# Weight-block sums made by accumulating loads: one step of a hybrid encoder layer

## The chip, the cores and the metric

The kernel runs on one core of one Trainium2 chip. A core has TensorE (PE) for matrix products, VectorE (DVE), ScalarE (ACT) and GpSimd (POOL) for everything else, SyncE (SP) for issuing transfers, and 16 DMA engines that carry them. The metric is the device time of one execution in microseconds. Before the change three runs took 2252.02, 2252.3 and 2253.97 us; the median is 2252.3 us.

## The reference: one layer of a streaming encoder

The input is x with 1024 frames of 1024 channels. One layer is computed, followed by a final RMSNorm:

1. h = RMSNorm(x), and one wide projection of h gives the columns for two branches. Branch A is a gated DeltaNet (8 heads of 128, short causal convolution, chunked delta rule). Branch B is gated linear attention, GLA (4 heads, keys of 128, values of 256, chunked). Each branch has a gated RMSNorm and a projection to 1024 channels, the two are merged by sigmoid gates, and an output projection adds the result to x.
2. x += cross attention of RMSNorm(x) over 256 memory tokens, 4 heads.
3. x += W2 relu(W1 RMSNorm(x))^2 with 4096 hidden channels.

All is float32. The large matrix products carry nearly all of the work: the projections of both branches, the output of the attention, and the two MLP products.

## The kernel before, in words

**Accuracy by splitting.** A float32 operand is split into a high half in a reduced type that TensorE takes at its fast rate (`fp32r`) and the rest, the low half. A product is then three matmuls: high by high, high by low, low by high (`mm3`, lines 487, 489 and 491). `split` does the splitting: ACT copies the high half (line 527), and DVE or POOL subtracts it from the raw value (line 528).

**Seven products for eight.** Many large products are done with Winograd's form of Strassen's scheme: both operands are taken as 2 x 2 blocks, and seven block products take the place of eight. For that, sums of blocks of both operands are needed, and sums of the results. The weight operand has blocks A11, A12, A21, A22, and the seven products use A11, A12, S2 = A21 + A22 - A11, S1 = A21 + A22, A22 - S2, A12 - S2 and A22. A *unit* is one such group of seven: per product 4 x 3 matmuls of 128x128 by 512 columns. `wino_w` (line 1551) prepares the weight operands of one unit, or of a pair of units: it makes four sums per unit, in place on the raw tiles (lines 1563, 1564, 1566 and 1568), and splits each into an operand tile. `wino` (line 1590) and `gla_dense` (line 861) issue the matmuls and hand the results to an `evict` function, which makes the sums of results out of PSUM: `into` (line 828), `sums` (line 1605) and `into_x` (line 1644). There are 39 units: 11 in the GLA stage (two of them with value weights in blocks of 256 columns), 8 for the two branch projections, 4 for the folded output of the attention, and 16 for the MLP's up projection.

**Tiles and rings.** Raw weights are loaded by SP into a ring of `RAWS = 4` tiles of 4 KB per partition named raw, and the split operands go into a ring of `RING = 4` tiles named wop. `queue_w` (line 1527) and `queue_gla` (line 1032) list the loads in order, `fetch_w` (line 1539) issues the next. A unit's raw tile holds 4 chunks of rows by 256 columns, so that a block is a strided half of it.

**The MLP's down projection** (`phase_mlp`, line 1964) is seven products over 15 chunks of rows, done in five passes: product 0, product 1, products 2 and 3, products 4 and 5, product 6. `weights` (line 2021) prepares one chunk of one pass, three steps ahead of the matmuls: for products 2 and 3 it loads blocks 0, 2 and 3, makes two sums (lines 2037 and 2038) and stores S2 to device memory (w2d); for products 4 and 5 it loads w2d and blocks 1 and 3 and makes two differences (lines 2043 and 2044). A step of two products is 24 matmuls of 512 columns.

**The order of the work.** The program is first written down as a plain trace, and a planner (`Plan`, line 131) then simulates all engines with a cost for each instruction and writes an order for each queue by list scheduling. An operation that adds or subtracts two tiles in SBUF may be moved between DVE and POOL by the planner (`Either`, line 399). A DMA costs 60 ns of its issuing engine there and lands after its bytes at 300 per ns plus 2600 ns (line 104). The queues of the engines are executed in the order that the planner wrote; only semaphores hold them back.

**Descriptors.** The kernel is built with `dynamic_dma_scratch_size=512` (line 2298), the bytes of each partition that are set aside for the descriptors of loads issued by GpSimd. Before the change there are no such loads.

Of the kernel before, what the change touches and what calls it, by code (L numbers as in the profile page):

```python
# [18 lines left out]
P = 128  # L19
# [54 lines left out]
class Op:  # L74
# [5 lines left out]
    def __init__(self, ins, flex):  # L80
# [343 lines left out]
class Layer:  # L424
# [206 lines left out]
    def phase0(self, xp):  # L631
        nc, a = self.nc, self.a
        with ExitStack() as ctx:
# [62 lines left out]
            def fold_o(h):  # L696
                vT = kv["wv"]
                w = [self.wpart(a["wo"][h][:, :, i * HALF:(i + 1) * HALF], [2, HALF], (None, nc.vector)[i], sp) for i in range(2)]
                for half in range(2):
                    for mb in range(2):  # L700
# [6 lines left out]
                        nc.scalar.activation(st.rearrange("p a b -> p (a b)"), pt, AF.Copy, scale=rm[0][:, mb:mb + 1])  # L707
                        nc.scalar.dma_start(self.Ud[:, 2 * half:2 * half + 2, mb, h], st)

# [118 lines left out]
    def into(self, dest, scale=1.0, done=None):  # L828

        nc = self.nc  # L830

        def add(o, pt, x):
            if scale == 1.0:
                nc.vector.tensor_tensor(o, pt, x, ADD)
            else:
                nc.vector.scalar_tensor_tensor(o, pt, scale, x, MUL, ADD)
# [690 lines left out]
    def queue_w(self):  # L1527
# [6 lines left out]
        q += [(4, [[g[:, 0:4], g[:, 4:8]]]) for g in self.Gd]  # L1534
        q += [(4, [[self.Ud[:, u, i] for i in range(2)] for u in us]) for us in pairs]
        q += [(4, [a["w1"][u] for u in us]) for us in [(0, 1)] + [(u,) for u in range(2, 14)] + [(14, 15)]]
        self.wq = deque(q)

    def fetch_w(self):
# [5 lines left out]
        for src in srcs:  # L1545
            rs.append([self.til(self.wp, [P, n, 256], "raw", bufs=RAWS) for _ in src])
            for t, x in zip(rs[-1], src):
                self.load(t, x)
        self.wr.append((n, rs))

    def wino_w(self, order, lov):

        nc, wp = self.nc, self.wp
        if not self.wr:
            self.fetch_w()
        n, rs = self.wr.popleft()
        ops = [{} for _ in rs]
        bl = [r if len(r) == 4 else [r[j][:, :, i * P:(i + 1) * P] for i in range(2) for j in range(2)] for r in rs]

        for p in order:  # L1560
            for o, (A11, A12, A21, A22) in zip(ops, bl):
                if p == 2:
                    nc.gpsimd.tensor_tensor(A21, A21, A22, ADD)
                    nc.gpsimd.tensor_tensor(A11, A21, A11, SUB)
                if p == 4:
                    nc.gpsimd.tensor_tensor(A21, A22, A11, SUB)
                if p == 5:
                    nc.gpsimd.tensor_tensor(A12, A12, A11, SUB)
                if A11.shape[-1] == P:
                    t = self.til(wp, [P, 2, n, P], "wop", F32R, bufs=RING)  # L1570
                    o[p] = t[:, 0], t[:, 1]
                else:
                    o[p] = [self.til(wp, [P, n, 256], "wop", F32R, bufs=RING) for _ in range(2)]
                self.split((A11, A12, A11, A21, A21, A12, A22)[p], *o[p], nc.vector if p in lov else None)
        return n, ops

    def plain_w(self):

        if not self.wr:
            self.fetch_w()  # L1580
        n, (r,) = self.wr.popleft()
        ops = {}
        for i in range(2):
            for j in range(2):
                t = ops[i, j] = self.til(self.wp, [P, 2, n, P], "wop", F32R, bufs=RING)
                self.split(r[j][:, :, i * P:(i + 1) * P], t[:, 0], t[:, 1])
        self.fetch_w()
# [17 lines left out]
    def sums(self, sp, done):  # L1605
# [6 lines left out]
        def evict(p, pt):  # L1612
# [9 lines left out]
            elif p == 2:  # L1622
                if "b" not in t:
                    t["b"] = self.til(sp, [P, HALF], "q", bufs=4)
                    nc.scalar.activation(t["b"], t["u"], AF.Copy)
                add(t["u"], pt, t["u"], ADD)
            elif p == 3:
# [16 lines left out]
    def into_x(self, sp, u, scale=1.0, done=None, tag="q", eng=None, up=None):  # L1644
# [16 lines left out]
        def evict(p, pt):  # L1661
# [8 lines left out]
            elif p == 2:  # L1670
                add(t["u"], pt, t["u"])
            elif p == 3:
# [291 lines left out]
    def phase_mlp(self, sp):  # L1964
# [56 lines left out]
        def weights(n):  # L2021
# [3 lines left out]
            ps, k = steps[n]  # L2025
            src = {(0,): "0", (1,): "1", (2, 3): "023", (4, 5): "S13", (6,): "3"}[ps]
            r = {}
            for i in range(0, len(src), 2):
                raw = self.til(self.wp, [P, 2, HALF], "raw", bufs=RAWS)
                for j, q in enumerate(src[i:i + 2]):  # L2030
                    r[q] = raw[:, j]
                    self.load(raw[:, j], self.w2d[k] if q == "S" else a["w2"][int(q), :, k])
            if len(src) == 1:
                ws = [r[src]]
            elif ps[0] == 2:

                nc.gpsimd.tensor_tensor(r["2"], r["2"], r["3"], ADD)
                nc.gpsimd.tensor_tensor(r["0"], r["2"], r["0"], SUB)
                nc.sync.dma_start(self.w2d[k], r["0"])
                ws = [r["0"], r["2"]]  # L2040
            else:

                nc.gpsimd.tensor_tensor(r["3"], r["3"], r["S"], SUB)
                nc.gpsimd.tensor_tensor(r["1"], r["1"], r["S"], SUB)
                ws = [r["3"], r["1"]]
# [103 lines left out]
    def run(self):  # L2149
# [5 lines left out]
        self.Gd = [dt([P, NB, 256], f"Gd{h}") for h in range(XH)]  # L2155
        self.Ud = dt([P, 4, 2, 4, 256], "Ud")
        self.md = [dt([P, 2, HALF], f"md{b}") for b in range(4)]
# [68 lines left out]
def _pairs(w):  # L2226

    return w.reshape(4, 2, P, -1, 256).transpose(3, 1, 2, 0, 4)

# [7 lines left out]
def _layout(i):  # L2237
# [9 lines left out]
                                             for h in range(LH)])])  # L2247
    A["w_lv"] = _pairs(w[:, lv])
    A["w_lr"] = _pairs(w[:, lr])
# [63 lines left out]
```

## Time and profile before

| | |
|---|---|
| median of three runs | 2252.3 us |
| lowest and highest | 2252.02 and 2253.97 us |
| span of the profiled execution, first to last instruction | 2248.6 us |
| median of the runs less that span | 3.7 us |
| TensorE busy | 2175.6 us, 97% |
| VectorE busy | 1668.2 us, 74% |
| ScalarE busy | 1101.5 us, 49% |
| GpSimd busy | 374.6 us, 17% |
| bytes moved by DMA | 300.20 MB, 134 GB/s on the mean |
| mean granted TensorE clock | 0.985 |

The profile is of one execution. Times are in us from the first instruction. A row of a group names the line of the kernel, the engine, the operation and its tiles (out<-in), their shape and the count; then come busy time and mean duration, or the shortest, median and longest duration. Matmuls are pipelined, so that the shown duration of one (0.39 us at 512 columns) is longer than the distance to the next. A row of waits says who waited for whom, how long in total, how often, and the longest. The landing time of a DMA is counted from its issue.

### The profile page before, as it was taken

The numbers are of one execution on the slowest core, as the hardware profiler recorded it, in microseconds if no ns is written. First come the engines' busy times: TensorE is split into PE (matmuls) and PEld (weight loads), VectorE is DVE, ScalarE is ACT, GpSimd is POOL, SyncE is SP. The second block draws the span as 40 slices with busy tenths as digits, with TensorE's granted clock in tenths as the row PEclk, the third lists the DMA queues.
The fourth block names the chain that finished last, engine by engine and source line by source line (L and its number), as shares of the span: only waits on it lengthen the run. The fifth ranks groups of instructions, "written<-read, shape, count | busy, mean of one in ns | idle before, by whom it ended". The sixth has DMA issues, their size and how long they took to land.

```text
span 2248.6 us, 32239 instructions
## 1 busy us (share of the span) xinstructions
PE 2175.6 (97%) x11552; PEld 1856.5 (83%) x11552; DVE 1668.2 (74%) x2901; ACT 1101.5 (49%) x2223; POOL 374.6 (17%) x326
## 2 busy tenths in 40 slices
PE   7899999989899999999998999999999999999996
PEld 7888979878788888888886888998888888888885
DVE  8836898687948858768558994558998778666756
ACT  6534554445445455355444433455665556544433
POOL 2100221022212222221111230002331002000012
PEclk9999999999999999999999999999999999999998
DMA  7932112122202102111167682244454445777732
GB/s 262 304 124 72 58 72 81 38 74 87 66 20 94 52 29 89 48 58 58 41 223 253 200 281 82 95 138 140 126 203 149 160 154 186 259 242 268 256 119 80
DMA packets 148463, 300.20 MB, mean 134 GB/s; under 512 B 15816, under 2 KB 22344, under 8 KB 148304
## 3 DMA queue, kind: packets, MB, share of 16 engines
q1 hardware_dynamic: 141504, 289.75, 38.6%
q10 hardware_dynamic: 6800, 8.42, 1.1%
q8 instruction: 90, 1.47, 0.3%
q14 instruction: 69, 0.57, 0.1%
HBM read 212.35 MB, written 85.75 MB: 133 GB/s over the span
## 4 chain that ended last, share of the span: by engine, by line
PE 83%; DVE 11%; issue 3%; ACT 2%; DMA 1%; POOL 0%; SPq 0%; DVEq 0%; ACTq 0%; POOLq 0%
PE pd L487 19%; PE pd L491 19%; PE pd L489 19%; PE ps L487 5%; PE ps L491 5%; PE ps L489 5%; PE ps L559 2%; DVE Pm L1223 1%; PE ps L1256 1%; DVE acc L1117 1%; DVE pr L1221 1%; PE ps L1247 1%; PE ps L1313 1%; PE ps L1296 1%; DVE wlo L528 1%
## 5 line engine op out<-in xcount | busy, mean ns | idle before, releaser
L527 ACT ACTIVATE wop<-raw 128x512 fp32r<-128x512 f32 (+1 forms) x444 | 297.1, 675 | 516.7 <-PE pd L491 242.9
L528 DVE TENSOR_TENSOR wop<-raw,wop 128x512 fp32r<-128x512 f32 (+1 forms) x387 | 297.3, 775 | 138.9 <-ACT wop L527 131.3
L1117 DVE SCALAR_TENSOR_TENSOR acc<-cin,convw,acc 128x1024 f32<-128x1024 f32 x72 | 96.8, 1345 | 7.9 <-ACT acc L1115 7.0
L527 ACT ACTIVATE whi<-raw 128x512 fp32r<-128x512 f32 x86 | 51.9, 627 | 92.3 <-PE pd L489 33.5
L528 POOL TENSOR_TENSOR wlo<-raw,whi 128x512 fp32r<-128x512 f32 x36 | 53.3, 1485 | 214.4 <-ACT whi L527 187.3
L491 PE MATMUL pd<-t,wop 128*128 128x512 f32 x220 | 88.9, 404 | 0.0
L487 PE MATMUL pd<-t,wop 128*128 128x512 f32 x220 | 86.9, 395 | 0.8 <-ACT t L527 0.8
L489 PE MATMUL pd<-t,wop 128*128 128x512 f32 x220 | 86.4, 393 | 0.7 <-DVE t L528 0.7
L491 PE MATMUL pd<-B1a,wop 128*128 128x512 f32 (+1 forms) x220 | 82.6, 376 | 0.0
L487 PE MATMUL pd<-B1a,wop 128*128 128x512 f32 (+1 forms) x220 | 82.6, 375 | 0.0
L528 POOL TENSOR_TENSOR wop<-raw,wop 128x512 fp32r<-128x512 f32 x23 | 33.0, 1434 | 271.2 <-ACT wop L527 260.5
L487 PE MATMUL pd<-A0a,whi 128*128 128x512 f32 x172 | 69.7, 405 | 0.0
L491 PE MATMUL pd<-A0a,wlo 128*128 128x512 f32 x172 | 69.0, 401 | 0.2 <-DVE wlo L528 0.2
L487 PE MATMUL pd<-A1b,whi 128*128 128x512 f32 x172 | 69.0, 401 | 0.0
L491 PE MATMUL pd<-A1b,wlo 128*128 128x512 f32 x172 | 68.6, 399 | 0.0
L489 PE MATMUL pd<-A1a,whi 128*128 128x512 f32 x172 | 68.6, 399 | 0.0
L489 PE MATMUL pd<-A0b,whi 128*128 128x512 f32 x172 | 68.2, 397 | 0.0
L487 PE MATMUL pd<-A1a,whi 128*128 128x512 f32 x172 | 68.1, 396 | 0.0
L491 PE MATMUL pd<-A1a,wlo 128*128 128x512 f32 x172 | 67.9, 395 | 0.0
L487 PE MATMUL pd<-A0b,whi 128*128 128x512 f32 x172 | 67.7, 393 | 0.0
L489 PE MATMUL pd<-A0a,whi 128*128 128x512 f32 x172 | 67.6, 393 | 0.0
L491 PE MATMUL pd<-A0b,wlo 128*128 128x512 f32 x172 | 67.6, 393 | 0.0
(623 smaller groups left out, 7163.3 us busy)
## 6 DMA issues: line engine op xcount, KB each, us to landing
raw<-in_w_dram SPq DMA_DIRECT2D x120, 256.0 KB, 3.5
raw<-in_w_gdn_dram SPq DMA_DIRECT2D x64, 256.0 KB, 2.7
raw<-in_w_dram SPq DMA_DIRECT2D x32, 512.0 KB, 4.0
e<-ad SPq DMA_DIRECT2D x63, 256.0 KB, 4.9
ad<-q SPq DMA_DIRECT2D x45, 256.0 KB, 2.8
rawa<-ad SPq DMA_DIRECT2D x42, 256.0 KB, 4.4
A0b<-tgd SPq DMA_DIRECT2D x32, 256.0 KB, 5.1
ad<-acc SPq DMA_DIRECT2D x30, 256.0 KB, 2.4
```

Of the source, the lines that this page charges most:

```text
L487: nc.tensor.matmul(out, lh, rh, start=first and i == 0, stop=False)
L489: nc.tensor.matmul(out, lh, rl, start=False, stop=False)
L491: nc.tensor.matmul(out, ll, rh, start=False, stop=last and i == n - 1)
L527: nc.scalar.activation(hi, raw, AF.Copy)
L528: (lo_eng or nc.gpsimd).tensor_tensor(lo, raw, hi.bitcast(F32), SUB)
L559: self.nc.tensor.transpose(pt[:, i * P:(i + 1) * P], s, self.ident)
L1117: nc.vector.scalar_tensor_tensor(acc, cin[:, 1 + i:1 + i + T], cw[:, i:i + 1], acc, MUL, ADD)
L1221: nc.vector.tensor_tensor(pr, X[:, c + 1:32, c:c + 1].broadcast_to([P, m, n]), Pm[:, c:c + 1, 0:n].broadcast_to([P, m, n]), MUL)
L1223: nc.vector.tensor_tensor(Pm[:, c + 1:32, 0:n], Pm[:, c + 1:32, 0:n], pr, ADD)
L1247: nc.tensor.matmul(pt[:, i * 96:(i + 1) * 96], NT[:, u + i, :], PF[:, v + i, 0:96], start=True, stop=True)
L1256: nc.tensor.matmul(pt[0:96, i * n:(i + 1) * n], PF[:, v + i, 0:96], Z, start=True, stop=True)
L1296: nc.tensor.matmul(py[:, 0:P], st["NT"][:, c, :], zh[h], start=True, stop=True)
```

## The change

Three of the four sums of weight blocks of a unit are no longer made by DVE or POOL but by a load that adds its source to what the tile holds, issued by GpSimd (`load_add`). A21 gets A22 added from device memory. S2 is made with the opposite sign, A11 - (A21 + A22), by the one sum that is left; A12 gets it added from SBUF; and A11 itself becomes operand 4 by adding A22 from device memory, where before A21 was overwritten. Because product 2 now has the opposite sign, the three evictions subtract it. In the down projection the sum of blocks 2 and 3 and the two differences are made in the same way; block 3 and the stored S2 are not loaded into tiles of their own any more, so that a step of two products needs one raw tile instead of two.

The arrays of weights are laid out by blocks of 128 columns, so that a block is one run of 2 KB per partition (4 KB for the GLA's value weights, which keep their layout), and the folded output weights (Ud) are stored accordingly. The planner counts 1000 ns of GpSimd for a DMA that GpSimd issues.

```diff
         if ins.opcode == "DMACopy":
-            self.dma, self.cost, self.lat = True, 60, 2600
+            self.dma, self.cost, self.lat = True, 1000 if eng == "gpsimd" else 60, 2600
...
-                        nc.scalar.dma_start(self.Ud[:, 2 * half:2 * half + 2, mb, h], st)
+                        nc.scalar.dma_start(self.Ud[:, mb, 2 * half:2 * half + 2, :, h].rearrange("p a b c -> p (a b) c"), st.rearrange("p a (b c) -> p (a b) c", c=P))
...
             elif p == 2:
-                add(u, pt, u)
+                add(u, pt, u, -scale)
...
+    def load_add(self, dst, src):
+        self.nc.gpsimd.dma_start(dst, src, accum_op=ADD)
...
-        n, rs = self.wr.popleft()
+        n, rs, srcs = self.wr.popleft()
         ops = [{} for _ in rs]
-        bl = [r if len(r) == 4 else [r[j][:, :, i * P:(i + 1) * P] for i in range(2) for j in range(2)] for r in rs]
+        quads = lambda r: r if len(r) == 4 else [r[j][:, i] for i in range(2) for j in range(2)]
+        bl, sl = [[quads(r) for r in q] for q in (rs, srcs)]
+        for (A11, A12, A21, A22), s in zip(bl, sl):
+            self.load_add(A21, s[3])
 
         for p in order:
-            for o, (A11, A12, A21, A22) in zip(ops, bl):
+            for o, (A11, A12, A21, A22), s in zip(ops, bl, sl):
                 if p == 2:
-                    nc.gpsimd.tensor_tensor(A21, A21, A22, ADD)
-                    nc.gpsimd.tensor_tensor(A11, A21, A11, SUB)
+                    nc.gpsimd.tensor_tensor(A11, A11, A21, SUB)
                 if p == 4:
-                    nc.gpsimd.tensor_tensor(A21, A22, A11, SUB)
-                if p == 5:
-                    nc.gpsimd.tensor_tensor(A12, A12, A11, SUB)
+                    if not 5 in o:
+                        self.load_add(A12, A11)
+                    self.load_add(A11, s[3])
+                if p == 5 and not 4 in o:
+                    self.load_add(A12, A11)
...
-                self.split((A11, A12, A11, A21, A21, A12, A22)[p], *o[p], nc.vector if p in lov else None)
+                self.split((A11, A12, A11, A21, A11, A12, A22)[p], *o[p], nc.vector if p in lov else None)
...
-            src = {(0,): "0", (1,): "1", (2, 3): "023", (4, 5): "S13", (6,): "3"}[ps]
+            src = {(0,): "0", (1,): "1", (2, 3): "02", (4, 5): "13", (6,): "3"}[ps]
...
-                    self.load(raw[:, j], self.w2d[k] if q == "S" else a["w2"][int(q), :, k])
+                    self.load(raw[:, j], a["w2"][int(q), :, k])
...
-                nc.gpsimd.tensor_tensor(r["2"], r["2"], r["3"], ADD)
-                nc.gpsimd.tensor_tensor(r["0"], r["2"], r["0"], SUB)
+                self.load_add(r["2"], a["w2"][3, :, k])
+                nc.gpsimd.tensor_tensor(r["0"], r["0"], r["2"], SUB)
                 nc.sync.dma_start(self.w2d[k], r["0"])
...
-                nc.gpsimd.tensor_tensor(r["3"], r["3"], r["S"], SUB)
-                nc.gpsimd.tensor_tensor(r["1"], r["1"], r["S"], SUB)
+                for q in "31":
+                    self.load_add(r[q], self.w2d[k])
...
-    return w.reshape(4, 2, P, -1, 256).transpose(3, 1, 2, 0, 4)
+    return w.reshape(4, 2, P, -1, 2, P).transpose(3, 1, 2, 4, 0, 5)
```

More of the change, by code (lines that the diff above doesn't have):

```diff
@@ L1534, in queue_w @@
         q += [(4, [[g[:, 0:4], g[:, 4:8]]]) for g in self.Gd]
-        q += [(4, [[self.Ud[:, u, i] for i in range(2)] for u in us]) for us in pairs]
+        q += [(4, [[self.Ud[:, i, u] for i in range(2)] for u in us]) for us in pairs]
         q += [(4, [a["w1"][u] for u in us]) for us in [(0, 1)] + [(u,) for u in range(2, 14)] + [(14, 15)]]
@@ L1585, in plain_w @@
                 t = ops[i, j] = self.til(self.wp, [P, 2, n, P], "wop", F32R, bufs=RING)
-                self.split(r[j][:, :, i * P:(i + 1) * P], t[:, 0], t[:, 1])
+                self.split(r[j][:, i], t[:, 0], t[:, 1])
         self.fetch_w()
@@ L1625, in evict @@
                     nc.scalar.activation(t["b"], t["u"], AF.Copy)
-                add(t["u"], pt, t["u"], ADD)
+                nc.vector.tensor_tensor(t["u"], t["u"], pt, SUB)
             elif p == 3:
@@ L1670, in evict @@
             elif p == 2:
-                add(t["u"], pt, t["u"])
+                nc.vector.scalar_tensor_tensor(t["u"], pt, -scale, t["u"], MUL, ADD)
             elif p == 3:
```

16 lines of the change are left out of this document (8 added, 8 removed).

## The prediction

> **What bounds the kernel now.** I read the page first, then the waits of TensorE, then the windows of the late stages, then the groups of the lines that the change touches.
>
> The page's first part, its queue table and its chain:
>
> ```profile
> span 2248.6 us, 32239 instructions
> PE 2175.6 (97%) x11552; PEld 1856.5 (83%) x11552; DVE 1668.2 (74%) x2901; ACT 1101.5 (49%) x2223; POOL 374.6 (17%) x326
> q1 hardware_dynamic: 141504, 289.75, 38.6%
> PE 83%; DVE 11%; issue 3%; ACT 2%; DMA 1%; POOL 0%; SPq 0%; DVEq 0%; ACTq 0%; POOLq 0%
> ```
>
> TensorE is busy for 2175.6 of 2248.6 us, so all that any change to the other engines can win is 73 us, and DVE at 74% is no bound by itself. The waits of TensorE say how much of the 73 us hangs on weight blocks:
>
> ```profile
> PE ps L1247 <- ACT PF L1233: 12.3, 4, 4.0
> PE ps L584 <- DVE rs_o L522: 8.7, 4, 3.3
> PE pd L487 <- ACT gst L707: 2.9, 1, 2.9
> PE ps L487 <- ACT B1b L527: 2.7, 2, 1.4
> PE pd L489 <- DVE B1a L528: 2.5, 1, 2.5
> PE pd L487 <- ACT wop L527: 1.1, 1, 1.1
> ```
>
> Columns: who waited for whom, us in total, times, longest. The largest waits belong to the gated-DeltaNet inverse (PF) and to the norms (rs_o). A weight operand (wop) was waited for once, 1.1 us. The sums that the change replaces feed wop and nothing else. The windows show where TensorE has room (columns: PE, PEld, DVE, ACT, POOL busy, clock, DMA share, GB/s):
>
> ```profile
> 1180.00:1290.00 110.00, 102.45 (x434) 81.52 (x434) 97.80 (x142) 50.36 (x88) 23.78 (x15) 0.98 0.67 227
> 1800.00:1880.00 80.00, 80.00 (x352) 65.79 (x351) 60.68 (x95) 41.84 (x68) 0.00 (x0) 1.00 0.45 155
> 2062.00:2144.00 82.00, 82.00 (x361) 67.42 (x360) 61.78 (x98) 34.16 (x61) 4.26 (x3) 1.00 0.72 240
> ```
>
> In the up projection (1800 to 1880) and the down projection (2062 to 2144) TensorE is full: nothing to win, only to lose. At the start of the merge (1180 to 1290) it stands idle for 7.5 us while DVE is 89% busy.
>
> **The sums removed.** Their groups, each with count and min/median/max ns:
>
> ```profile
> L1563 DVE TENSOR_TENSOR raw<-raw,raw x36: 674/684/1220, 158.4 to 1872.0; 128x512 f32<-128x512 f32 x34, 128x1024 f32<-128x1024 f32 x2
> L1563 POOL TENSOR_TENSOR raw<-raw,raw x3: 1278/1288/1755, 244.6 to 1671.6; 128x512 f32<-128x512 f32 x3
> L1566 DVE TENSOR_TENSOR raw<-raw,raw x39: 676/686/1796, 177.8 to 1891.3; 128x512 f32<-128x512 f32 x37, 128x1024 f32<-128x1024 f32 x2
> L1568 DVE TENSOR_TENSOR raw<-raw,raw x35: 677/684/1809, 185.4 to 1893.6; 128x512 f32<-128x512 f32 x33, 128x1024 f32<-128x1024 f32 x2
> L1568 POOL TENSOR_TENSOR raw<-raw,raw x4: 1295/1742/1748, 169.2 to 1618.0; 128x512 f32<-128x512 f32 x4
> L2037 DVE TENSOR_TENSOR raw<-raw,raw x15: 684/687/693, 1987.2 to 2063.9; 128x512 f32<-128x512 f32 x15
> L2043 DVE TENSOR_TENSOR raw<-raw,raw x15: 681/684/693, 2075.2 to 2143.7; 128x512 f32<-128x512 f32 x15
> L2044 DVE TENSOR_TENSOR raw<-raw x14: 683/686/695, 2070.1 to 2142.5; 128x512 f32<-128x512 f32 x14
> ```
>
> 39 units lose three sums each (117) and the 15 down steps of products 2 to 5 lose three (45): 162. DVE ran 154 of them (36 + 39 + 35 + 15 + 15 + 14), at 0.685 us about 105 us; POOL ran 8, some 11 us. Nearly all of it lay beside a full TensorE and is worth nothing, with one exception. In the merge these stood on DVE (time, us):
>
> ```profile
> 1183.67 0.69 DVE L1566 TENSOR_TENSOR raw<-raw,raw 128x512 f32<-128x512 f32 x1
> 1187.48 0.69 DVE L1568 TENSOR_TENSOR raw<-raw,raw 128x512 f32<-128x512 f32 x1
> 1188.08 0.69 DVE L528 TENSOR_TENSOR B1a<-e,B1a 128x512 fp32r<-128x512 f32 x1
> ```
>
> They are the first and the last of four sums ahead of the low half of B1a, for which TensorE waits 2.5 us. One starts 0.6 us after another, so four take 2.4 us: **-2.4 us**. Next late there is B1b, for which TensorE waits on ACT, not on DVE. Both ends: 0, and -7.5 if the whole idle time of the window went.
>
> **The loads added.** 162 accumulating loads are issued by POOL; 30 plain loads leave SP (block 3 and the stored sum are no longer loaded for themselves), 0.33 us of SP each. POOL's issue has no row here: bounds are SP's issue of 0.33 us and a POOL sum of 1.3 us, so 53 to 211 us on an engine that is 83% idle: 0 by itself. The transfer: q1 moved 141504 packets in 38.6% of 16 engines' 2248.6 us, 98 ns for one of 2 KB; 256 KB are 8 such on each engine, 0.79 us. An add reads the tile as well as the source, so I put it between 0.79 and 1.57 us. In the pass of products 4 and 5, a step today has five transfers (three weights, two activations), 3.9 us; then four plain ones and two adds, 4.7 to 6.3 us. The step's length is 24 matmuls, between the first of one and the first of the next:
>
> ```profile
> 2099.82 0.39 PE L487 MATMUL pd<-t,wop 128*128 128x512 f32 x1
> 2105.30 0.40 PE L487 MATMUL pd<-t,wop 128*128 128x512 f32 x1
> ```
>
> 5.48 us. Over 15 steps the upper end lacks 12 us, which the lead worked out below absorbs: 0. The Trainium skill (Collectives: The Full Stack, the section on the bandwidth ceiling) says that an add is slower because it needs two source reads, about half the rate; by it the 6.3 us would hold. No run here shows it yet.
>
> **Whether two such loads overlap.** This decides. The room for descriptors that GpSimd writes is 512 bytes of each partition (line 2298), and the page's queue table has no GpSimd queue at all, so the trace can't tell. Either two adds of a step go one behind the other at issue cost, or the second waits until the first has landed. What a landing takes, in that pass (the last two rows: first and last issue of the stored sum's load, and its landings):
>
> ```profile
> raw<-in_w_dram SPq DMA_DIRECT2D x31, 256.0 KB, 3.7
> raw<-w2d SPq DMA_DIRECT2D x14, 256.0 KB, 4.3
> e<-ad SPq DMA_DIRECT2D x12, 256.0 KB, 4.8
> L456 SPq DMA_DIRECT2D raw<-w2d x15: 319/320/385, 2062.6 to 2137.1; - x15
> DMA to landing us min/median/max: 2.0/4.4/6.6
> ```
>
> I take one at a time, because the room was set for a program without such loads and stays as it was, and 3.7 us each, the row with most loads of that size in that pass. The Trainium skill (DMA: Bandwidth & Descriptors, the section SWDGE vs HWDGE vs iDMA) says that GpSimd writes its descriptors into rings in SBUF, and its terms give 16 bytes for one; by it an estimate is room for 32 on an engine, and an add with two reads for each of 8 rows and one at the end is 17, so that two don't fit. Then two adds take 7.4 us of a 5.48 us step, and over 15 steps POOL falls 15 x 1.92 = 28.8 us behind. The lead that absorbs some of it: the pass begins about when product 3 has left PSUM for good,
>
> ```profile
> L1652 DVE TENSOR_TENSOR q<-ps,u x6: 681/682/683, 1549.8 to 2081.4; 128x512 f32<-128x512 f32 x6
> ```
>
> at 2081, 18.4 us after the first load of the stored sum (2062.6). A step now needs one raw tile of four instead of two, two further steps of lead, 11.0 us: 29.4. From it go a plain load (3.7), the two adds (7.4) and two splits (about 2): 16.3 us free. 28.8 - 16.3 = **+12.5 us**, near the end of the down projection, where nothing follows that could give it back. Both ends: 0 (at 2.0 us a landing the pair takes 4.0, under the step), and with 4.8 us 15 x 4.12 = 61.8, less 14.1 free, +48. The pass of products 2 and 3 has one add a step and stays under 5.48 us at any of these.
>
> **The chain inside a unit.** A12 gets A11 added, and after that A11 gets A22 added, so the split for product 4 lies behind two landings. In one unit of the up projection, the splits for products 1, 2 and 4 on ACT:
>
> ```profile
> 1793.34 0.63 ACT L527 ACTIVATE wop<-raw 128x512 fp32r<-128x512 f32 x1 [2.11 <-PE pd L491]
> 1796.11 0.63 ACT L527 ACTIVATE wop<-raw 128x512 fp32r<-128x512 f32 x1 [0.74 <-PE ps L491]
> 1802.04 0.62 ACT L527 ACTIVATE wop<-raw 128x512 fp32r<-128x512 f32 x1
> ```
>
> A split runs when a product of 2.74 us (half a step) leaves one of four operand tiles, so product 4 needs its own three products, 8.2 us, after its slot came free at about 1801.5: at 1809.7. The chain starts with the end of the split for product 1, low half included, at 1794.7. Two landings of 3.7 and a split of about 2 end at 1804.1; a third landing of the next unit's add between them makes it 1807.8. Hidden, **0**; it stops being hidden above 6.5 us a landing with two, above 4.3 us with three.
>
> What is queued behind: on POOL the add for A12 holds up the add for A11 and whatever low halves the planner left there, and ACT's split for product 4 holds up ACT's evictions behind it. POOL's own sums are 17% of the span, so I put nothing on it while the chain is hidden.
>
> **The rest.** The folded output weights are stored in pieces of 512 bytes instead of 1 KB. TensorE waits 2.9 us once for a staging tile (gst) that such a store frees; 0, at worst that wait doubled, +2.9. The three evictions with the changed sign are the same instruction on one operand order: 0. Weight loads keep 4 KB a partition: 0. One sum of four stays on its engine.
>
> **Sum.** The profiled execution: 2248.6 of span, 3.7 us below the runs' median of 2252.3; I put the same 3.7 around it after the change, and count from the median. 2252.3 - 2.4 (merge) + 12.5 (products 4 and 5) = 2262.4, say 2263.
>
> **The rivals.**
>
> *Hidden anyway.* Adds overlap, or land in under 2.7 us, half a step. Then only the merge moves: 2252.3 - 2.4 = 2250. For it: raw<-w2d has landings of 2.0 us among its 15, and 28% of the DMA time is free in the pass. Against it: the medians in that pass are 3.7 to 4.8. The Trainium skill (DMA: Bandwidth & Descriptors, Anatomy of one DMA) gives for a load issued by GpSimd 2.0 us and its bytes by 436 GB/s, by which 256 KB would take an estimated 2.6 us and this rival would hold; the plain loads of this trace are slower than that rule.
>
> *The chain of the units shows.* POOL passes one add at a time, landings are near e<-ad's 4.8 us, and an add for the next unit gets between the two of this one: 1794.7 + 14.4 + 2 = 1811.1, 1.4 us past 1809.7. There are 19 units with a single pair of raw tiles (3 of lqk, 4 of lr, 12 of the up projection): +27, 2277. For it: TensorE there has no slack at all, so every late operand counts. Against it: two landings alone leave 5 us of slack, and a planner that prices an add at 1.0 + 2.6 + 0.87 us (issue, latency, 256 KB at 300 bytes a ns, all in its code) keeps them apart.
>
> *Faster.* The one mechanism is DVE's relief at the start of the merge: if with DVE lighter the low halves of B1a, B1b and t follow their loads at once, up to 7.5 us of idle go, and the clock that was granted there (0.98) stays up: 2245. It decides from 4.5 us of them on. For it: DVE is 89% busy there. Against it: for B1b TensorE waits on ACT, and DMA share is already 0.67 there, to which six or more adds come.
>
> *Worse than my range.* Landings near the 6.6 us maximum: 15 x 7.7 less about 10 free is beyond +100. It needs each add at the slowest landing of the pass.
>
> **How the numbers follow.** One at a time with the last passes late: 45%, by its own ends of 3.5 to 4.8 us a landing 2256 to 2298. Hidden: 25%, 2248 to 2256. Units late as well: 12%, 2262 to 2290. Faster: 13%, 2241 to 2247.7. Beyond 2300: 5%. The likeliest gives the time, 2263. From 2246 to 2300 leaves out the last case and most of the faster one, under 2 in 10. Three runs before span 2 us, so 0.2%, 4.5 us, is about what can be told from no change: faster 0.14, same 0.27, slower 0.59.
>
> **What would show it.** POOL gets a DMA queue with 162 issues. Right: in the pass of products 4 and 5 ACT's splits wait for raw tiles that a POOL load wrote, TensorE waits for wop there some 10 us in all, mostly in the later steps, and two adds of a step start a landing apart. DVE loses about 105 us of busy time; the wait for B1a shrinks by 2 us. The up projection's windows stay at full TensorE. Wrong: two adds of a step issued 1 us apart with landings overlapping, or TensorE full from 2062 on (hidden); waits for wop in each up unit (the chain); or the loss outside the weights altogether, since the planner lays out all queues anew with the changed costs and may move a norm or an inverse by a few us either way.

## The result, and the profile after

The changed kernel takes 2357.95 us (median of four runs, 2356.43 to 2363.16), the kernel before 2252.16 us on the same chip. The ratio is 1.0481, with a 95% interval of 1.0467 to 1.0494: 106 us slower, far above the forecast of 2263 us and beyond the upper end of its range, 2300.

The page of the kernel after, its first part, its two large queues, its chain, and the two rows of its DMA issues that carry the most adds (count, size, median us to landing):

```profile
span 2354.4 us, 32617 instructions
PE 2208.9 (94%) x11552; PEld 1858.1 (79%) x11552; DVE 1584.0 (67%) x2751; ACT 1098.5 (47%) x2223; POOL 492.7 (21%) x476
q1 hardware_dynamic: 137184, 281.88, 35.5%
q0 software_dynamic: 23328, 44.05, 11.4%
PE 9%; DMA 9%; issue 5%; DVE 3%; ACT 1%; POOL 1%; SPq 0%; DVEq 0%; ACTq 0%; POOLq 0%
DMA raw<-in_w_dram 4%; DMA raw<-w2d 3%; PE pd L487 2%; PE pd L491 2%; PE pd L489 2%; PE ps L491 1%; PE ps L487 1%; PE ps L489 1%; DMA raw<-raw 1%; DVE wop L528 1%; ACT wop L527 1%; DMA rawa<-ad 1%; POOL wop L528 0%; DMA e<-ad 0%; POOL raw L1552 0%
raw<-in_w_dram POOLq DMA_DIRECT2D x47, 256.0 KB, 4.9
raw<-raw POOLq DMA_DIRECT2D x37, 256.0 KB, 3.8
```

The number of matmuls is the same, 11552, in a span that is 105.8 us longer. VectorE lost 84 us of work, and TensorE is busy for 94% of the span instead of 97%. What has changed is the chain that ended last. The two chains can't be compared share by share: the one before covers the whole span, while the one after is followed back only to 1696 us, so that its shares add up to 28%. Of these 28 points TensorE has 9, DMA 9, nearly all of it into the raw weight tiles, and "issue" 5; before, DMA had 1 of 100 and "issue" 3. In these last 658 us, transfers and waits before an issue hold more of the chain than TensorE does.

Who waits, on TensorE, on ACT and on POOL (one view for each engine; who waited for whom, us in total, times, longest):

```profile
PE pd L487 <- ACT wop L527: 30.6, 17, 7.7
PE pd L491 <- POOL wop L528: 12.8, 2, 11.7
PE ps L491 <- DVE wop L528: 10.8, 5, 3.0
PE ps L487 <- ACT wop L527: 9.1, 10, 1.5
...
ACT wop L527 <- DMA raw<-in_w_dram: 82.8, 16, 8.6
ACT wop L527 <- DMA raw<-w2d: 77.7, 24, 5.3
...
POOL raw L1552 <- issue: 229.0, 50, 45.2
```

Before, TensorE waited 1.1 us for a weight operand; the four largest rows for wop make 63.3 us now, and ACT's splits, which make these operands, wait in turn for the transfers that write raw. The last row is the one to learn from: POOL is about to issue an add, waits 229 us in all, and no tile, semaphore or engine that the profile shows releases it ("issue"). The longest of these waits, 45.2 us, stands before the very first add at 124.79 us, when none was in flight; the other 49 make 184 us. So semaphores are not all that holds a queue back here.

The timeline of POOL in the pass of products 4 and 5 shows what that is (start, us, instruction, idle before it and its releaser):

```profile
2191.78 0.87 POOL L1552 DMA_DIRECT2D raw<-w2d  x1 [3.71 <-issue]
2195.99 0.89 POOL L1552 DMA_DIRECT2D raw<-w2d  x1 [3.35 <-issue]
2200.16 0.88 POOL L1552 DMA_DIRECT2D raw<-w2d  x1 [3.28 <-issue]
2204.16 0.89 POOL L1552 DMA_DIRECT2D raw<-w2d  x1 [3.12 <-issue]
```

An issue takes 0.88 us, and the next comes 4.0 to 4.2 us after the last. The group of all adds of the down projection from w2d, and the landings of all adds of line 1552:

```profile
L1552 POOL DMA_DIRECT2D raw<-w2d x30: 862/875/898, 2117.1 to 2253.4; - x30
DMA to landing us min/median/max: 3.3/4.3/8.3
```

The distance of the issues is the landing time: each add waits until the one before it has landed. By the issue and landing times of the trace, none of the 162 adds is issued while another is in flight, and the earliest that one follows is 0.31 us after the landing before it. Thirty adds take (2253.4 - 2117.1) / 29 = 4.70 us each, 9.4 us for the two of a step, where the step's matmuls take 5.48.

The windows of four stages after (columns as in the prediction): start of the merge, up projection, products 2 and 3 with what stands around them, products 4 and 5.

```profile
1171.00:1340.00 169.00, 148.84 (x615) 116.97 (x614) 131.59 (x182) 67.24 (x117) 49.84 (x44) 0.97 0.87 271
1830.00:1910.00 80.00, 77.55 (x334) 61.82 (x333) 45.12 (x70) 34.47 (x59) 14.99 (x15) 1.00 0.65 184
1985.00:2100.00 115.00, 107.67 (x457) 86.69 (x456) 59.07 (x91) 44.50 (x78) 12.74 (x14) 0.98 0.76 217
2179.00:2261.00 82.00, 61.63 (x220) 40.63 (x219) 23.84 (x38) 21.34 (x37) 16.67 (x19) 0.96 0.65 151
```

In products 4 and 5 TensorE does 220 matmuls in 82 us, where it did 361 before. But the up projection isn't full either (334 in 80 us against 352), nor is the merge (TensorE busy for 148.84 of 169 us). The DMA engines are free for a third of the time in two of the four windows, so that it isn't their throughput that is short there.

### The profile page after: what moved, and what is told of

It reads as the page before. It is cut to its first block, busy times and chain, and to the rows that moved or that the text cites. A ratio compares the mean times of both kernels' runs of the same rounds, so it can differ in the third digit from the quotient of the medians.

```text
span 2354.4 us, 32617 instructions
## 1 busy us (share of the span) xinstructions
PE 2208.9 (94%) x11552; PEld 1858.1 (79%) x11552; DVE 1584.0 (67%) x2751; ACT 1098.5 (47%) x2223; POOL 492.7 (21%) x476
## 3 DMA queue, kind: packets, MB, share of 16 engines
q1 hardware_dynamic: 137184, 281.88, 35.5%
q0 software_dynamic: 23328, 44.05, 11.4%
## 5 line engine op out<-in xcount | busy, mean ns | idle before, releaser
L528 DVE TENSOR_TENSOR wop<-raw,wop 128x512 fp32r<-128x512 f32 (+1 forms) x380 | 307.5, 817 | 306.4 <-ACT wop L527 302.4
L487 PE MATMUL pd<-t,wop 128*128 128x512 f32 x220 | 90.4, 411 | 21.5 <-ACT wop L527 21.5
L1552 POOL DMA_DIRECT2D raw<-in_w_dram x47 | 41.4, 881 | 293.4 <-DMA raw<-in_w_dram 106.6
L491 PE MATMUL pd<-t,wop 128*128 128x512 f32 x220 | 91.8, 417 | 1.5 <-DVE wop L528 1.5
L489 PE MATMUL pd<-t,wop 128*128 128x512 f32 x220 | 88.5, 402 | 0.0
L1552 POOL DMA_DIRECT2D raw<-raw x39 | 34.6, 887 | 214.1 <-DVE wop L528 84.2
L491 PE MATMUL pd<-A1a,wop 128*128 128x512 f32 x164 | 67.0, 409 | 11.7 <-POOL wop L528 11.7
L528 POOL TENSOR_TENSOR wop<-raw,wop 128x512 fp32r<-128x512 f32 x30 | 55.8, 1871 | 95.4 <-ACT wop L527 84.5
L487 PEld LDWEIGHTS pd<-t,wop 128*128 128x128 f32 x220 | 42.7, 194 | 35.2 <-ACT wop L527 27.0
L487 PE MATMUL pd<-A0a,whi 128*128 128x512 f32 x172 | 69.6, 405 | 0.0
L489 PE MATMUL pd<-A0b,whi 128*128 128x512 f32 x172 | 68.7, 399 | 0.0
L489 PE MATMUL pd<-A1a,whi 128*128 128x512 f32 x172 | 68.4, 397 | 0.0
```

What stands on the lines that cost most here:

```text
L487: nc.tensor.matmul(out, lh, rh, start=first and i == 0, stop=False)
L489: nc.tensor.matmul(out, lh, rl, start=False, stop=False)
L491: nc.tensor.matmul(out, ll, rh, start=False, stop=last and i == n - 1)
L528: (lo_eng or nc.gpsimd).tensor_tensor(lo, raw, hi.bitcast(F32), SUB)
L1552: self.nc.gpsimd.dma_start(dst, src, accum_op=ADD)
```

## The experiments

The edits were made on the kernel after, by four switches that say where adds are used (GLA units, other units, products 2 and 3, products 4 and 5); where a switch is off, the sum is made by DVE or POOL as before, in the new layout. The switches move the lines: `load_add` is at line 1556 in most of these kernels, the split at 529 and 530. Times are medians; the kernel before took 2250.7 to 2251.3 us beside them. Where a text says that two kernels are paired by matmuls, the start times of the first, second, ... matmul of the two profiled executions are compared.

**More room for descriptors.**

```diff
-        nc = bacc.Bacc("TRN2", target_bir_lowering=False, num_devices=1, dynamic_dma_scratch_size=512)
+        nc = bacc.Bacc("TRN2", target_bir_lowering=False, num_devices=1, dynamic_dma_scratch_size=2048)
```

> The changed kernel with 2048 instead of 512 bytes of each partition for the descriptors of GpSimd's loads, nothing else. Theory: two adds don't fit the 512 bytes, so each waits for the landing of the one before (in the changed kernel they are issued 4.2 us apart). Then with room for several, the two adds of a step are issued about 0.9 us apart, the pass of products 4 and 5 goes from 8.4 us a step to between 5.5 and 6.3, and the whole falls by 40 us or more, to 2290 to 2320. Rival: GpSimd passes one add at a time whatever the room, or the data make it wait: issues stay 4 us apart and the time stays at 2350 to 2365.

Measured: 2249.14 us, ratio 1.0001 (0.9987 to 1.0015). The same 162 adds with the same bytes, in a program in which TensorE and SP carry out the same instructions in the same order, and the whole loss is gone, more than the theory had put on it (2290 to 2320): the loss in the units went with it. POOL's timeline in the pass of products 4 and 5, the group of its adds there with their landings, and a window over products 2 to 5:

```profile
2095.61 1.76 POOL L1556 DMA_DIRECT2D raw<-w2d  x2 [1.76 <-DVE A1a L530]
...
2116.12 2.65 POOL L1556 DMA_DIRECT2D raw<-w2d  x3 [1.51 <-DVE t L530]
...
DMA to landing us min/median/max: 4.8/7.4/10.3
...
1960.00:2120.00 160.00, 160.00 (x703) 131.50 (x702) 89.45 (x141) 67.13 (x116) 38.11 (x43) 1.00 0.97 274
```

Two and three adds are issued in one go, 0.88 us apart, and their landings overlap. One landing takes longer than before, 7.4 us on the median, with the DMA engines 97% busy, and yet TensorE is full for all 160 us. So the length of a landing does not decide; whether landings overlap does.

**Twice the room instead of four times.**

```diff
-dynamic_dma_scratch_size=512
+dynamic_dma_scratch_size=1024
```

> The changed kernel with 1024 bytes for descriptors. With 2048 the loss was gone. If an add takes 17 descriptors of 16 bytes on an engine (two reads for each of 8 rows and one at the end), 512 bytes hold one add and 1024 hold three: two adds of a step fit, issues 0.9 us apart in pairs, 2245 to 2260. If it takes more than 32 of the 64, one at a time as with 512: 2340 to 2365.

Measured: 2248.33 us, ratio 0.9992 (0.998 to 1.0004). POOL's timeline shows pairs again, one of them here:

```profile
2056.71 1.76 POOL L1552 DMA_DIRECT2D raw<-w2d  x2 [2.47 <-DMA raw<-in_w_dram]
```

1024 bytes are enough. By the issue and landing times of the traces, at most one add is in flight with 512 bytes, at most three with 1024 (24 of the 162 issues make it three), and up to five with 2048. This agrees with the prediction's estimate from the Trainium skill (DMA: Bandwidth & Descriptors, the sections Terms and SWDGE vs HWDGE vs iDMA; 17 descriptors of an add, 32 slots in 512 bytes: one fits; by the same terms three would fit in 1024). The count of slots itself no run shows.

**Layout alone.** All four switches off: no adds, the new layout of the weights, the changed sign of product 2 and the store of the folded output weights in smaller pieces stay.

```diff
-ADD_GLA, ADD_W, ADD_D23, ADD_D45 = True, True, True, True
+ADD_GLA, ADD_W, ADD_D23, ADD_D45 = False, False, False, False
```

> No accumulating loads at all: the four sums of a unit and of a down step are made by DVE or GpSimd as before the change; the layout by column block, the finer store of the folded weights and the opposite sign of product 2 stay. Theory (all the loss is the adds): 2245 to 2257. Rival (the layout or the new signs cost something, or the new plan does): above 2262.

Measured: 2241.6 us, ratio 0.9959 (0.994 to 0.9979): 10 us faster than before, and below what either theory had put. The new layout costs nothing, and the wait for gst L707 (2.9 us before) is not among TensorE's waits any more. The stores behind it did not get faster (their landings went from 6.0 to 7.4 us on the median); the planner's order around them is another one. By pairing the matmuls of the two traces in order, 3.6 us of the gain is there by 180 us of the span, 2 us come near 500 and 2 near 1550. This kernel is the base against which the adds are priced below; why each of these microseconds went was not followed further.

**Adds in the units alone, in the down projection alone.**

```diff
-ADD_GLA, ADD_W, ADD_D23, ADD_D45 = True, True, True, True
+ADD_GLA, ADD_W, ADD_D23, ADD_D45 = True, True, False, False
```

> Adds in the 39 units, sums in the down projection. By the stages of the two traces (up to the end of the up projection the changed kernel is some 33 us late, from -9 before the merge): theory of a chain behind each add: 2280 to 2295. Rival (the loss is in the down projection and the lateness before it is only carried by it): 2245 to 2262.

```diff
-ADD_GLA, ADD_W, ADD_D23, ADD_D45 = True, True, True, True
+ADD_GLA, ADD_W, ADD_D23, ADD_D45 = False, False, True, True
```

> Adds in the down projection alone, sums in the 39 units. By the stages of the two traces the down projection loses 70 us: theory 2310 to 2330. With the rival that adds of the units still in flight are what delays the down projection: below 2290.

Measured: units alone 2296.8 us (1.0201, 1.0147 to 1.0255), 55 us above the layout alone; down alone 2317.23 us (1.0292, 1.0262 to 1.0322), 76 us above it. Both halves lose, where I had put nothing on the units; the units lose a little more than their theory's upper end, 2295. Of the units alone there are only two runs, 10 us apart. The two make 131, the whole change 116 (2357.95 - 2241.6), so that they are not fully additive; why is not settled.

The windows of the units' kernel at the merge and at the first pair of units of the up projection, and then those of the layout alone:

```profile
1171.00:1340.00 169.00, 147.00 (x597) 115.36 (x595) 125.12 (x175) 65.13 (x112) 46.47 (x42) 0.95 0.87 267
1620.00:1700.00 80.00, 69.33 (x293) 55.09 (x292) 62.34 (x92) 47.74 (x83) 21.23 (x20) 0.96 0.61 161
1700.00:1900.00 200.00, 191.56 (x834) 154.06 (x833) 125.97 (x195) 93.47 (x160) 44.03 (x43) 0.99 0.67 182
```

```profile
1171.00:1340.00 169.00, 162.51 (x688) 130.21 (x687) 154.31 (x213) 73.13 (x125) 45.99 (x31) 0.98 0.74 245
1620.00:1700.00 80.00, 80.00 (x356) 65.69 (x354) 68.90 (x100) 51.69 (x88) 22.53 (x15) 1.00 0.57 199
1700.00:1900.00 200.00, 200.00 (x890) 164.91 (x891) 151.10 (x230) 110.88 (x184) 44.48 (x33) 1.00 0.48 160
```

At 0.228 us for a matmul (5.48 / 24) the 91 missing ones in the first row are 20.7 us, the 63 in the second 14.4, the 56 in the third 12.8. Paired by matmuls with the layout alone, the merge loses 24 us, the folded output and the first pair of the up projection 13, and the rest of the up projection, 12 single units and a pair, 23. So the pairs of units carry most of it, and the single units the rest. POOL's timeline in the merge of the kernel after shows where pairs lose: the first and the last of the six adds of its first pair, then three adds in a row of its last pair and the matmul that waited for them:

```profile
1155.79 0.96 POOL L1552 DMA_DIRECT2D raw<-in_w_bgla_dram  x1 [13.04 <-ACT wop L527]
...
1190.99 0.87 POOL L1552 DMA_DIRECT2D raw<-in_w_bgla_dram  x1 [4.68 <-DMA raw<-in_w_bgla_dram]
...
1307.96 0.89 POOL L1552 DMA_DIRECT2D raw<-raw  x1 [1.35 <-DVE u L1760]
1315.26 0.89 POOL L1552 DMA_DIRECT2D raw<-raw  x1 [6.40 <-DMA raw<-raw]
1321.41 0.88 POOL L1552 DMA_DIRECT2D raw<-in_w_bgdn_dram  x1 [5.26 <-issue]
...
1326.24 0.56 PE L487 MATMUL pd<-t,wop 128*128 128x512 f32 x1 [3.79 <-ACT wop L527]
```

In the first pair five distances take 35.2 us, 7.0 us each with the DMA engines 87% busy. Some rows name a tile or an engine as the releaser, but by the trace's landing times each of these adds goes out 0.3 us after the one before has landed. With the landing of the sixth, at 1195.53, they take 39.7 us, and the pair's 14 products of 2.74 us are 38.4 us of matmuls: one at a time there is no room to spare. In the last pair the third add is issued 13.5 us after the first and lands at 1325.45; ACT's split and TensorE's wait of 3.8 us follow. In a pair such a split stands behind three landings, where the prediction reckoned with two of 3.7 us in a single unit, three at most. There, between 1310 and 1320 us of the layout's own time, the kernel after loses 9 of the 17 us that the merge costs it.

**Products 2 and 3 alone, products 4 and 5 alone.**

```diff
-ADD_GLA, ADD_W, ADD_D23, ADD_D45 = True, True, True, True
+ADD_GLA, ADD_W, ADD_D23, ADD_D45 = False, False, True, False
```

> 512 bytes, adds in the pass of products 2 and 3 alone, sums elsewhere. In the kernel with adds in the whole down projection that pass is some 27 us longer though it has one add a step. Theory (one add at a time, 4.9 us to land plus its issue, behind a plain load that SP sends late, is itself longer than a step of 5.48 us): 2258 to 2275. Rival (the pass loses because the adds for products 4 and 5 stand in the same queue): 2238 to 2250.

```diff
-ADD_GLA, ADD_W, ADD_D23, ADD_D45 = True, True, True, True
+ADD_GLA, ADD_W, ADD_D23, ADD_D45 = False, False, False, True
```

> 512 bytes, adds in the pass of products 4 and 5 alone. Two adds of 4.2 us against a step of 5.48: 15 steps lose 44 us less some lead. Theory: 2270 to 2290. Rival (most of that loss is carried over from the pass before): below 2260.

Measured: products 4 and 5 alone 2305.46 us (1.025, 1.0216 to 1.0284), 64 us above the layout alone; products 2 and 3 alone 2258.01 us (1.0037, 1.0022 to 1.0052), 16 us above it. The first lies 15 us above the upper end of its theory, 2290; the second only just inside its own. By pairing matmuls with the layout alone, the second kernel is late by 12.4 us in its profiled execution, all of it inside that pass; the first by 65 us, all of it inside its pass. In the kernel after, the same pairing gives 47 us up to products 2 and 3 (the units), 12 us in products 2 and 3, 55 us in products 4 and 5.

The adds of products 4 and 5 in the first of these kernels, and the splits on ACT at the beginning of that pass:

```profile
L1556 POOL DMA_DIRECT2D raw<-w2d x30: 872/884/1068, 2061.3 to 2207.6; - x30
ACT wop L529: 115.3, 28
DMA to landing us min/median/max: 3.9/4.2/8.5
...
2068.86 0.63 ACT L529 ACTIVATE wop<-raw 128x512 fp32r<-128x512 f32 x1 [7.47 <-DMA raw<-w2d]
2073.23 0.63 ACT L529 ACTIVATE wop<-raw 128x512 fp32r<-128x512 f32 x1 [3.74 <-DMA raw<-w2d]
...
2073.91 0.50 PE L489 MATMUL ps<-A1b,wop 128*128 128x512 f32 x1 [0.67 <-ACT wop L529]
```

The second row says that ACT's splits waited for 28 of the 30 adds. The adds are (2207.6 - 2061.3) / 29 = 5.04 us apart, 10.1 us for the two of a step. Already the second split of the pass is late: TensorE waits for it at 2073.91. There is next to no lead: the first add is issued at 2061.3, and the second has landed only 12 us later. Over 15 steps the deficit is 15 x (10.1 - 5.48) = 69 us, less some 5 us: the 64 that were measured.

In products 2 and 3 there is one add a step. POOL's timeline of the kernel with these alone, and the landings of its adds:

```profile
2003.35 0.89 POOL L1556 DMA_DIRECT2D raw<-in_w_dram  x1 [5.88 <-DMA e<-ad]
2010.77 0.88 POOL L1556 DMA_DIRECT2D raw<-in_w_dram  x1 [6.53 <-issue]
...
2029.65 0.89 POOL L1556 DMA_DIRECT2D raw<-in_w_dram  x1 [7.20 <-DMA raw<-in_w_dram]
2037.21 0.88 POOL L1556 DMA_DIRECT2D raw<-in_w_dram  x1 [6.67 <-DMA raw<-in_w_dram]
...
DMA to landing us min/median/max: 4.7/5.4/7.9
```

From 2003.35 to 2037.21 five steps take 6.8 us each, and over the whole pass they take 6.5, against the 5.48 of the matmuls. Most of that is the add itself: its landing has a median of 5.4 us and a mean of 5.8, longer than a step, and ten of the fourteen distances end 0.3 us after the landing before. In the other four POOL stood for 0.7 to 2.6 us after that landing; the rows name other transfers there and once a tile. In the same stretch SP stands at the head of its queue on the store of S2, which waits for the sum:

```profile
SPq L2060 <- DVE raw L2059: 45.1, 13, 7.9
```

**The store of S2 from another queue.** Because SP issues all plain loads, that wait looked like a loop: load, add, sum, store, and only then the next load. ACT issues the store here, with 512 bytes and all adds.

```diff
-                nc.sync.dma_start(self.w2d[k], r["0"])
+                nc.scalar.dma_start(self.w2d[k], r["0"])
```

> 512 bytes again, and the store of S2 in the pass of products 2 and 3 is issued by ACT instead of SP. In the changed kernel SP stood 48 us ahead of that store, waiting for the sum behind the add, with the next weight loads queued behind it. Theory that this blocking makes the loss of that pass (some 24 us): 2330 to 2345. Rival (the adds themselves, one at a time and interleaved with those for products 4 and 5 on GpSimd, set the pace): 2350 to 2365.

Measured: 2366.24 us, ratio 1.0517 (1.0489 to 1.0545), no better than the kernel after and 1 us above the rival's range. With the store off SP's queue the time did not go down, so the theory that its place on SP makes the loss in products 2 and 3 is not borne out. But the wait has only moved: now ACT stands behind the sum, and in that stretch splits of the other operand (t, B0a, B1b, A1a) wait 19.8 us for it. What a store that blocks no queue would give is not shown.

**A higher price for the planner.** The planner books 1.0 us of GpSimd for an add and lets it land later. Here it is told that the add holds GpSimd until it has landed. That is stricter than the trace: what has to wait is the next add, while a subtraction that stands before it starts during the flight (at 2147.38 us, 0.57 us after an add, in rows shown further below).

```diff
-            self.dma, self.cost, self.lat = True, 1000 if eng == "gpsimd" else 60, 2600
+            self.dma, self.cost, self.lat = True, 4100 if eng == "gpsimd" else 60, 100 if eng == "gpsimd" else 2600
```

> 512 bytes again, and the planner is told what was measured: an add holds GpSimd 4.1 us and lands 1.0 us after that, instead of 1.0 and 3.5. Theory (room for one add is the bound in the down projection, order is second): the units lose less, the pass of products 4 and 5 stays at two adds of 4.2 us a step: 2310 to 2345. Rival (the loss is mostly a bad order from a wrong price): below 2290.

Measured: 2366.69 us, ratio 1.0519 (1.0487 to 1.055). Both theories had put a gain here and miss. Paired by matmuls with the kernel after, it is 15 us later in the profiled executions: it loses 5 us before the merge and 12 from there to the up projection's first pair, wins some 10 in the rest of the up projection and 5 in products 2 and 3, and loses 13 from products 4 and 5 to the end. So this price gives no better order. A planner that counts adds in flight as something apart from GpSimd's time was not tried.

**Adds in the GLA's units, with room.** With 2048 bytes, and adds only in the 11 units of the GLA stage, where VectorE is busiest: can the relief of VectorE win anything once the adds overlap?

```diff
-ADD_GLA, ADD_W, ADD_D23, ADD_D45 = True, True, True, True
+ADD_GLA, ADD_W, ADD_D23, ADD_D45 = True, False, False, False
...
-dynamic_dma_scratch_size=512
+dynamic_dma_scratch_size=2048
```

> 2048 bytes, adds in the 11 units of the GLA stage alone, sums everywhere else, the new layout. By the stages of the runs with room and with the layout alone, adds with room save some 3 to 6 us up to the merge and lose some 8 after it: theory 2234 to 2242, below both kernels and at or below the layout alone. Rival (that saving is the accident of one plan): 2242 to 2252.

Measured: 2243.84 us, ratio 0.9968 (0.9958 to 0.9977). It falls in the rival's range. It is faster than both kernels of the change, but not below the layout without any add (0.9959, 0.994 to 0.9979; the intervals overlap), so nothing shows a gain that would be the adds'. The layout alone has the lowest median of all that ran.

## Why the prediction was wrong, by its own steps

**One add at a time: right, and it decided.** The prediction took it that two adds don't overlap in 512 bytes. The issues one landing apart, and the return to 1.0001 and 0.9992 with more room, show it. Its stated sign, two adds of a step starting a landing apart and ACT's splits waiting for tiles that a POOL load wrote, is in the rows above. The size of that sign was not: some 10 us of waits for wop had been put for products 4 and 5, and the rows above make 63.3 us in the whole kernel.

**"Then two adds take 7.4 us of a 5.48 us step": mis-sized.** The term was 3.7 us an add, the median landing of the plain loads in that pass. Measured were 4.70 us from issue to issue in the kernel after and 5.04 with the adds there alone; the landing itself has a median of 4.0 to 4.2 us there. The median was not far off; but a sum over 30 adds goes by their mean, 4.4 to 4.7 us, and 0.3 us pass from a landing to the next issue. Two adds take 9.4 to 10.1 us, and the deficit is 59 to 69 us in place of 28.8. My upper end, 4.8 us (the row of e<-ad), lay nearer.

**"16.3 us free": wrong.** The lead was counted from the first load of the stored sum (2062.6) to 2081 us, when product 3 leaves PSUM for good, plus two steps for the raw tiles that come free, 29.4 us in all. But the pass begins before product 3 has left PSUM. In the kernel before, the first matmul of product 4 is this one:

```profile
2077.83 0.40 PE L487 MATMUL pd<-A1a,wop 128*128 128x512 f32 x1
```

That is 15.2 us after the first load, not 18.4. And in the run with these adds alone the pass begins at 2070.26, 8.9 us after its first add at 2061.33: the freed raw tiles brought no lead at all. Its two first adds take 11.9 us up to the second split, so that TensorE waits in the first step. What kept the first add from being issued earlier is not shown. Some 5 us of the deficit were absorbed. By these two steps +12.5 became +64.

**"The pass of products 2 and 3 has one add a step and stays under 5.48 us": wrong.** It cost 16 us. I had compared an add of at most 4.8 us with the step; in that pass it lands after 5.4 us on the median and 5.8 on the mean, and the adds came 6.5 us apart.

**"Hidden, 0" for the chain inside a unit: wrong.** It cost 55 us. The check was made on a single unit of the up projection, with its two adds behind the split of product 1, and stopped at the latency of the chain. The pairs of units, where six adds take 39.7 us beside 38.4 us of matmuls and a split stands behind three landings, were left out, though the same count (adds of a unit, times a landing, against the unit's matmuls) had been made for products 4 and 5. And the landings were taken from the down projection's plain loads at 3.7 us, while adds in the merge land after 5.5 us on the median. The rival "the chain of the units shows" was right in kind at +27; it too counted the 19 single units and left the pairs out. Of its 19 the seven of the GLA stage cost nothing that is left at 1150 us, where the kernel with adds in the units alone is 0.2 us late.

**POOL's queue.** The prediction named the low halves on POOL as what is queued behind an add, and put nothing on it. The longest wait of TensorE, 11.7 us, is one of them:

```profile
2117.15 0.88 POOL L1552 DMA_DIRECT2D raw<-w2d  x1 [5.12 <-DMA raw<-in_w_dram]
...
2146.81 0.87 POOL L1552 DMA_DIRECT2D raw<-w2d  x1 [3.35 <-issue]
2147.38 1.59 POOL L528 TENSOR_TENSOR wop<-raw,wop 128x512 fp32r<-128x512 f32 x1
```

From the first row to the last but one POOL issued seven adds of the pass of products 4 and 5, two for each step. The low half belongs to the first block of the second step, whose add was the third (2129.86 us); ACT made the high half at 2134.11. Four further adds stand ahead of it, at 2134.32, 2138.46, 2142.58 and 2146.81 us, one landing apart, and three of them are for later steps. POOL takes its queue in order, so that TensorE waited for a subtraction of 1.6 us until adds had gone out that nobody needed yet.

**The transfer: a little above its bounds.** A packet of q0 takes 11.4% x 16 x 2354.4 / 23328 = 0.184 us, one of q1 35.5% x 16 x 2354.4 / 137184 = 0.097 us. With 23328 / 162 = 144 packets an add, 9 on each engine, an add is 1.66 us of the DMA engines, where I had put 0.79 to 1.57. The rule of two source reads at about half the rate (the Trainium skill, Collectives: The Full Stack, the section on the bandwidth ceiling) agrees with these 0.184 against 0.097 us. It was absorbed: with room, TensorE is full at 97% DMA share.

**The rest.** The issue of an add takes 0.88 us, between the bounds of 0.33 and 1.3. DVE lost 84 us of the 105 expected. The layout and the store cost nothing, as put; that their new plan would be 10 us faster was not foreseen. At the start of the merge the wait for B1a on DVE fell from 2.5 us as put, with this row in the kernel after:

```profile
PE pd L489 <- DVE B1a L528: 0.8, 1, 0.8
```

But the adds lose there far more than the 1.7 us that it gives. The rival of 2245 is not borne out: with room, where VectorE is as much relieved (1572.8 us of work), the time is that of before, and the layout with all its sums on the engines is faster. The rival "hidden" (2250) is what happens with 1024 or 2048 bytes. Its condition was that adds overlap, and the rule that a load issued by GpSimd takes 2.0 us plus its bytes by 436 GB/s (the Trainium skill, DMA: Bandwidth & Descriptors, Anatomy of one DMA), an estimate of 2.6 us here, is not borne out: in the kernel after the shortest landing of an add is 3.3 us, the median 4.3.

## What to carry to other kernels

Before work is moved into transfers that one engine issues, find out how many of them may be in flight; if it is one, multiply the count of transfers in each stage by a whole landing, at its mean in that stage, and hold it against that stage's matmuls, for every stage and for its densest unit, not only for the one that looks worst. Count too how many landings stand behind one operand. An engine that stands idle with "issue" as its releaser, with issues one landing apart, is the sign of it. The sums removed here cost VectorE time beside a nearly full TensorE, and removing them won nothing that the runs show, so that the change had only a price.

## What the runs showed of the hardware that was not expected

With 512 bytes of each partition for GpSimd's descriptors, one add of 256 KB was in flight at a time, and the next was issued 0.3 us after its landing at the earliest. The adds were 4.7 to 5.0 us apart in products 4 and 5, 6.5 in products 2 and 3, and 7.0 in the first pair of the merge, and what stood behind an add in GpSimd's queue waited with it. With 1024 bytes issues came 0.88 us apart with up to three adds in flight, and 110 us (2357.95 to 2248.33) went with a change of one number.

With more adds in flight each landed later (7.4 us on the median with 2048 bytes against 4.0 with 512, in products 4 and 5), and it cost TensorE nothing: it is busy for all of 160 us at 97% DMA share.
